# Projections and gated merge of a hybrid decoder block, walked in halves of the tokens instead of in columns of both halves

## The chip, the cores and the metric

The kernel runs on one core of one Trainium2 chip. The metric is device time in microseconds (us) of one execution; a comparison uses the median of several. The engines that matter here are TensorE (PE, with its weight loads PEld), VectorE (DVE), ScalarE (ACT), GpSimd (POOL) and SyncE (SP); SP does no arithmetic here and issues most of the transfers, POOL issues others. Each engine works through its own list of instructions in order: an instruction that waits holds up everything behind it on that engine, the transfers that it would issue included.

## The reference

One decoder block over 1024 tokens of width 1024, in float32:

```python
h = rmsnorm(x, norm1_g)
proj = h @ w_in                       # q, k, v, then u and v of the gating unit, then two gates
gate_a = sigmoid(proj[..., A]); gate_b = sigmoid(proj[..., B])        # 1024 columns each
attn = ...   # dilated attention, three groups mixed: 512 columns
sgu  = ...   # spatial gating unit: 512 columns
merged = gate_a * (attn @ w_proj_attn) + gate_b * (sgu @ w_proj_sgu)  # 512 x 1024 weights each
x = x + merged @ w_out
x = x + (silu(h2 @ w_ffn_gate) * (h2 @ w_ffn_up)) @ w_ffn_down        # h2 = rmsnorm(x, norm2_g)
return rmsnorm(x, final_g)
```

The change concerns the line `merged = ...` and the end of the computation of the two gates just before it.

## The kernel before, in words

Every float32 operand of a product is split into a high part, rounded to the format that TensorE multiplies, and a low part, the rest. `split` (L103 to L105) is one ACT copy (L104, CAST in the profile) and one DVE subtraction (L105). A product takes three matmuls per 128 rows of contraction: high by high, high by low, low by high.

**Gates.** The two gates (8 columns of 128 for each, called c) are computed for both halves of the tokens (512 tokens each) by a scheme that needs seven products in place of eight for each c (`seven`, L803 to L850, driven by the list `order`). A product (c, i) is 12 matmuls of 512 columns. Products 1, 6 and 7 copy their running PSUM sum to a tile `sn` by an ACT copy (L850) before the next product adds to the same bank, which therefore waits for that copy. `gates_after` (L892 to L914) forms the gate values on DVE (L912 among others), applies the sigmoid on ACT (L893) and writes each finished gate, 512 KB for each c and gate, to DRAM by POOL's queue (`put`, L801, in the traces `gate<-go`). Gate weights arrive in tiles `gr`, a ring of 6. On PE the stage ends, as the scheduler placed it, with the products (7,6), (7,5), (7,3) in a bank Z of its own, (7,7) and (7,4).

**Operands of the projections.** The gating unit's output (`sgud`) and the attention's (`attd`) lie in DRAM. `load_side(side, half)` (L940) fetches one side and half in two tiles of 512 KB through SP's queue, and `split_side` (L949) splits them: three of the four (side, half) pairs into the tile `HX`, whose three blocks have been operands of the gate products and come free one after the other, the last pair into a tile `at1` that is made when the merge begins. They pass through the tiles `raw`, a ring of 3.

**Merge.** For each of 8 columns c, for each side (0 is the gating unit, 1 the attention), for each half, there is one projection product: 4 rows of contraction by 3 matmuls, 12 matmuls in a PSUM bank `acc` (3 banks), by `cols_mm` (L351; matmuls on L357 to L359). There are 32 such products. A weight piece ("p", side, c), 256 KB, is loaded by SP into a `raw` tile (L137) and split into a slot of the ring `WH`/`WL`, 8 slots of 512 columns (`need`, `pump`, `load_jobs`); it serves both halves. `load_sg` (L990) fetches both gates of a column, 512 KB each, from DRAM through POOL's queue (L994), one column ahead. DVE multiplies a PSUM bank by the gate (L1006 for side 0, L1008 for side 1), which frees the bank, adds (L1009), and the sum is split into `H`, the left operand of the product with `w_out`, which comes next (matmuls on L344 to L346).

**What sets the order.** A scheduler places each engine's instructions, by the written order, the dependences and `issue_after`, which holds an instruction behind another one. Tiles of one tag share a fixed number of places (`BUFS`); a new tile waits until the old one in its place is no longer used. Pools that open later take the memory of closed ones, so a first write into the new pool also waits for the last use of what lay there: the gate values `sg` lie where gate weights and `go` tiles lay.

## Time and profile before

| What | Value |
|---|---|
| Time, median of 3 runs | 1695.07 us (1692.18 to 1696.88) |
| Profiled execution | 1696.83 us, its span 1695.1 us |
| Mean granted TensorE clock | 0.992 |
| PE busy | 1658.6 us, 98% of the span, 8110 matmuls |
| DVE, ACT, POOL busy | 995.5 us (59%), 709.2 us (42%), 239.4 us (14%) |
| Merge (first to last matmul of L357 to L359) | 856.77 to 957.15 us |

The profile is one execution. A row of a timeline reads: start in us, duration in us, engine, line, operation, tile written and tiles read, repeats, and in brackets the idle time before it on that engine and what ended it. PE's rows begin every 0.23 us though each lasts 0.39, because matmuls overlap; so the time between two starts, not the sum of durations, is what a product costs. A row of windows reads: window, its length, busy time and count for PE, PEld, DVE, ACT and POOL, then the granted TensorE clock, the mean busy share of the 16 DMA engines, and the bytes that they moved in GB/s. Which engine is busiest over the whole says little on one stage; what ended each idle time of PE says where the time can go.

### The profile page before, as it was taken

Reading aid. Unit: us, or ns where it says so; the run is one execution under the profiler, and the core shown is the slowest. Engines: PE = TensorE matmul, PEld = TensorE weight load, DVE = VectorE, ACT = ScalarE, POOL = GpSimd, SP = SyncE. Lnnn points to the kernel's source line nnn. Section 1 sums busy time; section 2 is a strip of 40 time slices with the busy share of each in tenths; the row PEclk is TensorE's granted clock in tenths of the full one; section 3 lists DMA queues with packets and bytes.
Section 4 is the critical chain, followed back from the end, with each engine's and each line's share of the span. In section 5 each row is a group of like instructions: output and inputs, shape, how many; then the busy total and the mean of one; then the engine's idle time right before and its main releaser. Section 6 shows DMA issues by size and latency. Waiting matters only on the chain.

```text
span 1695.1 us, 22401 instructions
## 1 busy us (share of the span) xinstructions
PE 1658.6 (98%) x8110; PEld 1346.8 (79%) x8110; DVE 995.5 (59%) x1868; ACT 709.2 (42%) x1383; POOL 239.4 (14%) x417
## 2 busy tenths in 40 slices
PE   8999999999999999999979999999999999999998
PEld 7877877877887778778858888888888888888886
DVE  5365376366447694665456428776566555565555
ACT  5345435435444563544342116433333333354444
POOL 6200030030012045021010002021000000100003
PEclk9999999999999999999989999999999999999999
DMA  7312331152232224576375514365332322496663
GB/s 216 92 42 70 85 103 50 30 151 55 55 115 75 65 100 132 166 267 224 130 238 179 173 38 149 131 223 190 113 106 95 100 93 94 157 338 231 197 190 111
DMA packets 196239, 227.55 MB, mean 134 GB/s; under 512 B 14561, under 2 KB 141921, under 8 KB 196129
## 3 DMA queue, kind: packets, MB, share of 16 engines
q1 hardware_dynamic: 156624, 135.30, 25.9%
q0 software_dynamic: 24144, 81.38, 13.7%
q10 hardware_dynamic: 15360, 9.45, 2.4%
q8 instruction: 64, 1.05, 0.3%
q14 instruction: 47, 0.38, 0.1%
HBM read 159.52 MB, written 63.41 MB: 132 GB/s over the span
## 4 chain that ended last, share of the span: by engine, by line
PE 60%; issue 9%; DMA 3%; DVE 3%; ACT 1%; POOL 1%; SPq 0%; ACTq 0%; POOLq 0%; DVEq 0%
PE ps_X L845 4%; PE ps_X L847 4%; PE ps_X L846 4%; PE ps_acc L345 4%; PE ps_acc L346 4%; PE ps_acc L344 4%; PE ps_acc L357 3%; PE ps_acc L358 3%; PE ps_acc L359 3%; PE ps_V L847 2%; PE ps_V L846 2%; PE ps_V L845 2%; PE ps_dX L1231 2%; PE ps_dX L1230 2%; PE ps_dX L1229 2%
## 5 line engine op out<-in xcount | busy, mean ns | idle before, releaser
L344 PE MATMUL ps_acc<-WH,H 128*128 128x384 f32 (+1 forms) x512 | 190.6, 374 | 3.6 <-ACT H L104 3.6
L346 PE MATMUL ps_acc<-WH,H 128*128 128x384 f32 (+1 forms) x512 | 191.1, 374 | 0.5 <-DVE H L105 0.5
L345 PE MATMUL ps_acc<-WL,H 128*128 128x384 f32 (+1 forms) x512 | 189.8, 371 | 0.0
L104 ACT CAST WH<-rows 128x512 fp32r<-128x512 f32 x132 | 81.8, 621 | 207.5 <-PE ps_X L846 97.8
L104 ACT CAST WH<-raw 128x512 fp32r<-128x512 f32 (+2 forms) x105 | 85.4, 817 | 178.6 <-PE ps_V L846 48.1
L105 DVE TENSOR_TENSOR WL<-rows,WH 128x512 fp32r<-128x512 f32 x132 | 90.9, 690 | 115.5 <-ACT WH L104 115.5
L359 PE MATMUL ps_acc<-H,WL 128*128 128x512 f32 x384 | 154.0, 401 | 0.0
L357 PE MATMUL ps_acc<-H,WH 128*128 128x512 f32 x384 | 153.8, 400 | 0.0
L358 PE MATMUL ps_acc<-H,WH 128*128 128x512 f32 x384 | 153.3, 399 | 0.0
L845 PE MATMUL ps_X<-H,WH 128*128 128x512 f32 x360 | 141.7, 394 | 3.8 <-ACT sn L850 2.2
L846 PE MATMUL ps_X<-H,WH 128*128 128x512 f32 x360 | 141.5, 393 | 0.0
L847 PE MATMUL ps_X<-H,WL 128*128 128x512 f32 x360 | 138.0, 392 | 0.0
L105 DVE TENSOR_TENSOR WL<-raw,WH 128x512 fp32r<-128x512 f32 (+2 forms) x105 | 97.5, 930 | 42.6 <-ACT WH L104 42.2
L462 ACT ACTIVATE S<-S,sm 128x128 f32<-128x128 f32 (+1 forms) x192 | 84.8, 444 | 70.9 <-DVE sm L460 62.3
L344 PEld LDWEIGHTS ps_acc<-WH,H 128*128 128x128 f32 x512 | 97.1, 190 | 16.4 <-ACT H L104 4.2
L346 PEld LDWEIGHTS ps_acc<-WH,H 128*128 128x128 f32 x512 | 96.9, 189 | 12.6 <-issue 0.9
L345 PEld LDWEIGHTS ps_acc<-WL,H 128*128 128x128 f32 x512 | 96.9, 189 | 11.9 <-issue 0.7
L846 PE MATMUL ps_V<-HX,WH 128*128 128x512 f32 x232 | 91.2, 393 | 0.0
L845 PE MATMUL ps_V<-HX,WH 128*128 128x512 f32 x232 | 91.1, 393 | 0.0
L847 PE MATMUL ps_V<-HX,WL 128*128 128x512 f32 x232 | 91.0, 392 | 0.0
L105 DVE TENSOR_TENSOR WL<-ab,WH 128x512 fp32r<-128x512 f32 x74 | 51.0, 689 | 59.2 <-ACT WH L104 59.2
L359 PEld LDWEIGHTS ps_acc<-H,WL 128*128 128x128 f32 x384 | 72.6, 189 | 16.3 <-issue 0.3
(297 smaller groups left out, 3630.9 us busy)
## 6 DMA issues: line engine op xcount, KB each, us to landing
raw<-in_w_in_dram SPq DMA_DIRECT2D x32, 512.0 KB
raw<-in_w_ffn_down_dram POOLq DMA_DIRECT2D x22, 512.0 KB, 5.3
twd<-raw POOLq DMA_DIRECT2D x22, 512.0 KB, 3.0
rows<-in_w_ffn_gate_dram SPq DMA_DIRECT2D x22, 512.0 KB
rows<-in_w_ffn_up_dram SPq DMA_DIRECT2D x22, 512.0 KB
ab<-twd SPq DMA_DIRECT2D x44, 256.0 KB
gr<-in_w_in_dram SPq DMA_DIRECT2D x16, 512.0 KB
gate<-go POOLq DMA_DIRECT2D x16, 512.0 KB, 4.9
```

Source lines behind the costliest of these rows:

```text
L104: marks["hi"] = nc.scalar.copy(hi, src)
L105: return tt(out=lo, in0=src, in1=fb(hi), op=ALU.subtract)
L344: mm(o, H[:, 0, kt, tok], wh, start=(kt == 0), stop=False)
L345: mm(o, H[:, 0, kt, tok], wl, start=False, stop=False)
L346: mm(o, H[:, 1, kt, tok], wh, start=False, stop=(kt == KT - 1))
L357: mm(ps, WH[:, w], rh, start=(kt == 0), stop=False)
L358: mm(ps, WH[:, w], rl, start=False, stop=False)
L359: mm(ps, WL[:, w], rh, start=False, stop=(kt == n - 1))
L462: nc.scalar.activation(sbt[:, o:o + n], sbt[:, o:o + n], AF.Exp, bias=neg[:, i:i + 1], scale=0.125, accum_out=stt[:, b, 2 + h:3 + h])
L845: mm(ps, WH[:, w], OPS[i](0, k), start=first and k == 0, stop=False, skip_group_check=True)
L846: mm(ps, WH[:, w], OPS[i](1, k), start=False, stop=False, skip_group_check=True)
L847: mm(ps, WL[:, w], OPS[i](0, k), start=False, stop=k == 3, skip_group_check=True)
```

## The change

The merge's loops now run half, then column, then side. Each weight piece is loaded and split once for each half (32 jobs of 256 KB in place of 16). The gate values come as one tile for each half and column that holds both gates, 256 KB each, three steps ahead with four places; those of the first two steps go through SP's queue, placed ahead of the weight pieces that follow, the others stay on POOL's. The operands of half 0 are fetched earlier, into places of the gate weights' ring `gr`, while the last ten products of the gates run; the operands of half 1 are fetched into two tiles `side` in the fourth and sixth step of the merge (n is 3 and 5), and split in the sixth and eighth: the attention's is side 1 with half 1, and takes over the block of `HX` that side 0 of half 0 leaves free. There is no tile `at1`. The first four weight pieces are split before the merge begins. Some `issue_after` orders are added: the operands of side 1 behind those of side 0, splits of later pieces behind the last sum and sigmoid of the gates.

```diff
@@ -72,7 +72,7 @@
     dram = ctx.enter_context(tc.tile_pool(name="dram", bufs=1, space=bass.MemoryType.DRAM))
 
     BUFS = {"A": 4, "qkr": 2, "cs": 2, "vst": 3, "vp": 2, "oT": 3, "att": 2, "raw": 3, "S": 2, "pT": 2, "st": 6,
-            "sm": 8, "cmb": 2, "x2": 8, "y": 2, "sn": 5, "e": 3, "yo": 4, "ab": 6, "go": 4, "gr": 6, "side0": 8, "side1": 8, "sg": 4, "mg": 2, "c": 5}
+            "sm": 8, "cmb": 2, "x2": 8, "y": 2, "sn": 5, "e": 3, "yo": 4, "ab": 6, "go": 4, "gr": 6, "side": 2, "sg": 4, "mg": 2, "c": 5}
     PBUFS = {"acc": 3, "tr": 2, "s": 2, "o": 1, "X": 3, "Y": 2, "V": 2, "Z": 1, "dX": 4, "dV": 3, "dv": 1}
     BASE = {"H", "WH", "WL", "ident", "mhalf", "raw", "sm", "bsT"}
     first_pool = open_pool("mixer")
@@ -121,7 +121,7 @@
     jobs = []
     piece = {}
     live = {}
-    stat = {"load": 0, "split": 0, "at": 0, "raws": 2, "limit": 1 << 30}
+    stat = {"load": 0, "split": 0, "at": 0, "raws": 2, "limit": 1 << 30, "behind": ()}
     raws = {}
     RING = 4096
     AHEAD = 6
@@ -133,8 +133,11 @@
         while stat["load"] < min(len(jobs), stat["limit"]) and stat["load"] < stat["split"] + stat["raws"]:
             key, dmas, shape, n = jobs[stat["load"]]
             t = T_("raw", shape)
-            for dst, src in dmas(t):
-                nc.sync.dma_start(out=dst, in_=src)
+            with ExitStack() as behind:
+                if "sg" in marks:
+                    behind.enter_context(tc.issue_after(marks["sg"].ins))
+                for dst, src in dmas(t):
+                    marks["job"] = nc.sync.dma_start(out=dst, in_=src)
             raws[key] = (t, cur[0])
             stat["load"] += 1
 
@@ -151,7 +154,10 @@
         flat = t if len(shape) == 2 else t.rearrange(f"p {names} -> p ({names})")
         a, ok = room(n)
         assert ok, key
-        split(WH[:, a:a + n], WL[:, a:a + n], flat)
+        with ExitStack() as behind:
+            for ins in stat["behind"]:
+                behind.enter_context(tc.issue_after(ins))
+            split(WH[:, a:a + n], WL[:, a:a + n], flat)
         live[key] = (a, n)
         piece[key] = a
         stat["at"] = a + n
@@ -327,9 +333,10 @@
         for kp in range(4):
             job(("uv", which, kp), one(w_in2[:, 2 * kp:2 * kp + 2, c0:c0 + SGW]), [P, 2, SGW], 1024)
     stat["limit"] = len(jobs)
-    for c in range(KT):
-        for side, wp in enumerate((wps, wpa)):
-            job(("p", side, c), one(wp[:, :, c * P:(c + 1) * P]), [P, 4, P], 512)
+    for half in range(2):
+        for c in range(KT):
+            for side, wp in enumerate((wps, wpa)):
+                job(("p", half, side, c), one(wp[:, :, c * P:(c + 1) * P]), [P, 4, P], 512)
     for ch in range(2):
         for kp in range(4):
             job(("o", ch, kp), one(wo[:, 2 * kp:2 * kp + 2, half_of(ch)]), [P, 2, 512], 1024)
@@ -905,11 +912,11 @@
             if c < KT - 2:
                 load_wd(c, "raw")
         if i == 4:
-            sig(go[c, 0][:, t1], ps)
+            marks["sig"] = sig(go[c, 0][:, t1], ps)
             put(gates_d[0][c], go.pop((c, 0)))
         if i == 3:
             o = go.pop((c, 1))
-            tt(out=o[:, t0], in0=o[:, t0] if last else snap[c, 6], in1=ps, op=ALU.add)
+            marks["add"] = tt(out=o[:, t0], in0=o[:, t0] if last else snap[c, 6], in1=ps, op=ALU.add)
             sig(o[:, t0], o[:, t0])
             put(gates_d[1][c], o)
 
@@ -934,12 +941,12 @@
 
 
     side_raw = {}
-    side_at = {(0, 0): HX[:, 1], (0, 1): HX[:, 0], (1, 0): HX[:, 2]}
+    side_at = {(0, 0): HX[:, 1], (1, 0): HX[:, 0], (0, 1): HX[:, 2], (1, 1): HX[:, 1]}
     side_op = lambda side: lambda kt, half: (side_at[side, half][:, 0, kt], side_at[side, half][:, 1, kt])
 
     def load_side(side, half):
         for q in range(2):
-            t = side_raw[side, half, q] = T_("raw", [P, 2, 512])
+            t = side_raw[side, half, q] = T_("side" if half else "gr", [P, 2, 512])
             if side == 0:
                 nc.sync.dma_start(out=t, in_=sgud[:, 2 * q:2 * q + 2, half_of(half)])
             else:
@@ -950,24 +957,25 @@
         dst = side_at[side, half]
         for q in range(2):
             kk = slice(2 * q, 2 * q + 2)
-            split(dst[:, 0, kk], dst[:, 1, kk], side_raw.pop((side, half, q)))
+            marks["lo"] = split(dst[:, 0, kk], dst[:, 1, kk], side_raw.pop((side, half, q)))
 
     for n, (c, i) in enumerate(order):
         left = len(order) - n
         if n + AHEAD_W < len(order):
             weights(*order[n + AHEAD_W])
-        if left == 7:
-            load_side(0, 0)
-            stat.update(limit=len(jobs), raws=1)
-            load_jobs()
+        if left in (10, 9):
+            load_side(10 - left, 0)
         if left == 4:
             split_side(0, 0)
-            load_side(0, 1)
+            parts = marks["hi"], marks["lo"]
+            stat.update(limit=stat["limit"] + 4, raws=3)
+            load_jobs()
         if left == 3:
+            with tc.issue_after(parts[0].ins), tc.issue_after(parts[1].ins):
+                split_side(1, 0)
             stat["at"] = ring[0] % 8 * 512
-            need(("p", 0, 0))
-        if left == 2:
-            split_side(0, 1)
+            for key in (("p", 0, 0, 0), ("p", 0, 1, 0), ("p", 0, 0, 1), ("p", 0, 1, 1)):
+                need(key)
         product(c, i)
         if i == 7:
             load_gates(c + 3)
@@ -978,36 +986,50 @@
     merge_pool = open_pool("merge")
     PBUFS["tr"] = 5
     merge_psum = open_pool("merge_psum", bass.MemoryType.PSUM)
-    side_at[1, 1] = T_("at1", [P, 2, 4, 512], F32R)
-    T_("pad", [P, 512])
-    load_side(1, 0)
-    split_side(1, 0)
-    load_side(1, 1)
-    split_side(1, 1)
-    stat["raws"] = BUFS["raw"]
+    T_("pad", [P, 4608])
+    stat.update(limit=len(jobs), behind=(marks["sig"].ins, marks["add"].ins))
     sg = {}
 
-    def load_sg(c):
-        if c < KT:
-            sg[c] = [T_("sg", [P, S]) for _ in range(2)]
-            for j in range(2):
-                nc.gpsimd.dma_start(out=sg[c][1 - j], in_=gates_d[1 - j][c])
-
-    load_sg(0)
-    for c in range(KT):
-        load_sg(c + 1)
-        m = T_("mg", [P, S])
-        for side in range(2):
-            for half in range(2):
+    def load_sg(n):
+        if n < 2 * KT:
+            half, c = divmod(n, KT)
+            sg[n] = T_("sg", [P, 2, 512])
+            for j in (1, 0):
+                queue = nc.sync if n < 2 else nc.gpsimd
+                load = queue.dma_start(out=sg[n][:, j], in_=gates_d[j][c][:, half_of(half)])
+                if n < 2:
+                    marks["sg"] = load
+
+    for n in range(BUFS["sg"] - 1):
+        load_sg(n)
+    load_jobs()
+    for half in range(2):
+        for c in range(KT):
+            n = KT * half + c
+            load_sg(n + BUFS["sg"] - 1)
+            if n == 2:
+                stat["behind"] = ()
+                del marks["sg"]
+            if n == 3:
+                with tc.issue_after(marks["job"].ins):
+                    load_side(0, 1)
+            if n == 5:
+                with tc.issue_after(marks["hi"].ins), tc.issue_after(marks["mg"].ins):
+                    split_side(0, 1)
+                load_side(1, 1)
+            m = T_("mg", [P, 512])
+            for side in range(2):
                 pp = PS("acc")
-                cols_mm(pp, ("p", side, c), 4, side_op(side), half, half == 1)
-                gt, mh = sg[c][1 - side][:, half_of(half)], m[:, half_of(half)]
+                cols_mm(pp, ("p", half, side, c), 4, side_op(side), half, True)
+                gt = sg[n][:, 1 - side]
                 if side == 0:
-                    tt(out=mh, in0=gt, in1=pp, op=ALU.mult)
+                    tt(out=m, in0=gt, in1=pp, op=ALU.mult)
+                    if n == KT - 1:
+                        split_side(1, 1)
                 else:
                     tt(out=gt, in0=gt, in1=pp, op=ALU.mult)
-                    tt(out=mh, in0=mh, in1=gt, op=ALU.add)
-                    split(H[:, 0, c, half_of(half)], H[:, 1, c, half_of(half)], mh)
+                    tt(out=m, in0=m, in1=gt, op=ALU.add)
+                    marks["mg"] = split(H[:, 0, c, half_of(half)], H[:, 1, c, half_of(half)], m)
     close_pool(merge_pool)
     close_pool(extra_pool)
 
```

PE has the same matmuls in both kernels. The first place where the order of the other engines moves is SP's queue from the last gate weights on. Here L944 and L947 (L951 and L954 of the changed kernel) fetch operands, L137 (L140) a weight piece, L999 gate values. Before:

```order
L944 DMA raw_1014_7385<-sgud_5306 128x2x512
L944 DMA raw_1015_7387<-sgud_5306 128x2x512
L137 DMA raw_1016_7389<-in_w_proj_sgu_dram 128x4x128
L944 DMA raw_1020_7442<-sgud_5306 128x2x512
L944 DMA raw_1021_7444<-sgud_5306 128x2x512
L137 DMA raw_1023_7461<-in_w_proj_attn_dram 128x4x128
L947 DMA raw_1029_7525<-attd0_81 128x512
...
L947 DMA raw_1032_7538<-attd3_84 128x512
L137 DMA raw_1040_7577<-in_w_proj_sgu_dram 128x4x128
```

After:

```order
L951 DMA gr_1010_7327<-sgud_5306 128x2x512
L951 DMA gr_1011_7329<-sgud_5306 128x2x512
L954 DMA gr_1014_7356<-attd0_81 128x512
...
L954 DMA gr_1015_7359<-attd3_84 128x512
L140 DMA raw_1021_7446<-in_w_proj_sgu_dram 128x4x128
L140 DMA raw_1022_7448<-in_w_proj_attn_dram 128x4x128
L140 DMA raw_1023_7450<-in_w_proj_sgu_dram 128x4x128
L140 DMA raw_1025_7471<-in_w_proj_attn_dram 128x4x128
L999 DMA sg_1030_7536<-gate1_0_6317 128x512
...
L999 DMA sg_1031_7539<-gate0_1_6310 128x512
L140 DMA raw_1033_7545<-in_w_proj_sgu_dram 128x4x128
```

Both lists begin behind the last load of gate weights. In the second, half 0's operands and four weight pieces come first, then the gate values of two steps; the twelve transfers of operands of the first list are six, and the other half's follow later.

The second place is ACT around the two copies to `sn` (L850, L857 of the changed kernel) that the last two products of the gates wait for. Before:

```order
L893 ACTIVATE go_1011_7341<-go_1011_7341 128x512
L104 CAST HX_909_6350<-raw_1014_7385 128x1024
L850 COPY sn_1019_7436<-ps_X_1012_7352 128x512
L104 CAST HX_909_6350<-raw_1015_7387 128x1024
L850 COPY sn_1024_7475<-ps_X_1012_7352 128x512
```

After:

```order
L900 ACTIVATE go_1013_7345<-go_1013_7345 128x512
L104 CAST HX_909_6350<-gr_1010_7327 128x1024
L104 CAST WH_2_67<-raw_1025_7471 128x512
L857 COPY sn_1020_7440<-ps_X_1016_7362 128x512
L104 CAST HX_909_6350<-gr_1011_7329 128x1024
L104 CAST HX_909_6350<-gr_1014_7356 128x1024
L104 CAST HX_909_6350<-gr_1015_7359 128x1024
L857 COPY sn_1026_7491<-ps_X_1016_7362 128x512
```

The casts of operands stand around the copies in both; in the second they read `gr` tiles, and a weight piece's cast stands ahead of the first copy.

The third place is DVE where the gates end and the merge begins: L1006, L1008 and L1009 (L1026, L1030 and L1031) are the merge's multiplications and addition. Before:

```order
L912 TENSOR_TENSOR go_1025_7477<-go_1025_7477,ps_Z_1026_7485 128x512
L105 TENSOR_TENSOR WL_3_68<-raw_1023_7461,WH_2_67 128x512
L105 TENSOR_TENSOR HX_909_6350<-raw_1029_7525,HX_909_6350 128x1024
L105 TENSOR_TENSOR HX_909_6350<-raw_1030_7528,HX_909_6350 128x1024
L105 TENSOR_TENSOR at1_1027_7523<-raw_1031_7535,at1_1027_7523 128x1024
L105 TENSOR_TENSOR at1_1027_7523<-raw_1032_7538,at1_1027_7523 128x1024
L105 TENSOR_TENSOR WL_3_68<-raw_1040_7577,WH_2_67 128x512
L1006 TENSOR_TENSOR mg_1037_7553<-sg_1034_7546,ps_acc_1038_7554 128x512
```

After:

```order
L919 TENSOR_TENSOR go_1027_7493<-go_1027_7493,ps_Z_1028_7497 128x512
L1026 TENSOR_TENSOR mg_1037_7554<-sg_1030_7536,ps_acc_1038_7555 128x512
L1030 TENSOR_TENSOR sg_1030_7536<-sg_1030_7536,ps_acc_1039_7569 128x512
L1031 TENSOR_TENSOR mg_1037_7554<-mg_1037_7554,sg_1030_7536 128x512
L1026 TENSOR_TENSOR mg_1044_7601<-sg_1031_7539,ps_acc_1045_7602 128x512
L105 TENSOR_TENSOR H_1_66<-mg_1037_7554,H_1_66 128x512
L105 TENSOR_TENSOR WL_3_68<-raw_1033_7545,WH_2_67 128x512
```

Before, six splits stand between the gates' last sum and the merge's first multiplication, the last of them that of a weight piece; now the first multiplication follows the gates' last sum, and the first split of a weight piece comes after three multiplications.

## The prediction

> **What bounds the kernel now.** I read the page first, then PE's waits, then windows and timelines around the largest wait. PE's first row of the page and the head of its waits:
>
> ```profile
> PE 1658.6 (98%) x8110; PEld 1346.8 (79%) x8110; DVE 995.5 (59%) x1868; ACT 709.2 (42%) x1383; POOL 239.4 (14%) x417
> PE ps_acc L357 <- DVE mg L1006: 9.8, 1, 9.8
> ...
> PE ps_X L845 <- ACT sn L850: 2.2, 3, 0.8
> ```
>
> PE bounds the kernel, and the change leaves its matmuls as they are; only PE's waits, and half-clock stretches behind them, can be won. One wait stands out: a merge matmul (L357) waited 9.8 us, once, for the first multiplication by a gate (L1006). PE's timeline from the last gate products to the first product with `w_out`:
>
> ```profile
> 849.01 0.40 PE L847 MATMUL ps_Z<-HX,WL 128*128 128x512 f32 x1
> 850.22 0.50 PE L845 MATMUL ps_X<-H,WH 128*128 128x512 f32 x1 [0.81 <-ACT sn L850]
> 852.85 0.39 PE L847 MATMUL ps_X<-H,WL 128*128 128x512 f32 x1
> 853.91 0.50 PE L845 MATMUL ps_X<-H,WH 128*128 128x512 f32 x1 [0.68 <-ACT sn L850]
> 856.77 0.40 PE L357 MATMUL ps_acc<-HX,WH 128*128 128x512 f32 x1
> 864.79 0.40 PE L359 MATMUL ps_acc<-HX,WL 128*128 128x512 f32 x1
> 874.95 0.77 PE L357 MATMUL ps_acc<-at,WH 128*128 128x512 f32 x1 [9.76 <-DVE mg L1006]
> 880.21 0.43 PE L357 MATMUL ps_acc<-HX,WH 128*128 128x512 f32 x1
> 957.15 0.39 PE L344 MATMUL ps_acc<-WH,H 128*128 128x512 f32 x1
> ```
>
> From 880.21 to 957.15 run 28 of the 32 merge products: 76.94 / 28 = 2.748 us each, 0.229 per matmul. By that pace the Z product could have been followed at 849.24, and two gate products and 32 merge products would take 34 x 2.748 = 93.43 us; they took 957.15 - 849.24 = 107.91. So 14.5 us are lost here, and no more can be won: 850.22 - 849.24 = 0.98 before (7,7); 0.83 before (7,4), 853.91 less 852.85 + 0.23; 0.11 in each of these two products, slow to start (853.91 to 856.77 is 2.86); 874.95 - 865.02 = 9.93, where 865.02 is 864.79 + 0.23, the end of three products, as many as there are banks; and the fourth product, 874.95 to 880.21, 5.26 - 2.75 = 2.51 too long. The windows say why that product is long, and what the DMA engines did (clock, DMA share and GB/s are the last three numbers):
>
> ```profile
> 865.00:868.00 3.00, 0.19 (x1) 0.00 (x0) 1.23 (x1) 0.61 (x2) 0.53 (x1) 1.00 1.03 407
> 868.00:872.00 4.00, 0.00 (x0) 0.00 (x0) 1.23 (x1) 0.96 (x1) 0.00 (x0) 0.76 1.05 386
> 875.00:878.00 3.00, 3.00 (x7) 2.40 (x8) 2.88 (x5) 1.24 (x3) 0.53 (x1) 0.50 0.62 145
> 880.00:957.00 77.00, 77.00 (x337) 63.13 (x337) 47.50 (x71) 17.77 (x27) 6.34 (x12) 1.00 0.51 155
> ```
>
> After the gap PE had half its clock (0.50); during it all 16 DMA engines were full. The chain of waits tells what L1006 waited for:
>
> ```profile
> 862.48 10.36 DMA raw<-in_w_proj_sgu_dram
> 872.86 0.63 ACT WH L104
> 874.12 0.69 DVE mg L1006
> ```
>
> The multiplication's own inputs were not the last to come: it stood in DVE's order behind the split of the third weight piece, whose 256 KB took 10.36 us through the full DMA engines. And the piece was asked for only at 862.48, since its `raw` tile went through two rounds of operands first.
>
> **The change part by part.** *The 9.93 us.* In the new order of DVE the first multiplication stands directly behind the gates' last sum, and four pieces are split before. It then hangs on its gate values. The rows on them:
>
> ```profile
> 849.05 0.53 POOL L801 DMA_DIRECT2D gate<-go  x1 [5.69 <-ACT go L893]
> 858.45 1.05 POOL L801 DMA_DIRECT2D gate<-go  x2 [8.87 <-ACT go L893]
> 866.61 0.53 POOL L994 DMA_DIRECT2D sg<-gate  x1 [5.53 <-DMA gate<-go]
> gate<-go POOLq DMA_DIRECT2D x16, 512.0 KB, 4.9
> DMA to landing us min/median/max: 3.7/4.8/10.6
> ```
>
> The last row is of the tile `sg`, 512 KB a load. The first `sg` tile now lies where the second-last column's `go` lay, so its load needs that `put` landed: 849.05 + 4.9 = 853.95 at the latest if nothing else moves, some 2 us sooner if its sigmoid no longer stands behind a cast of operands (below). The merge would start at 856.77 - 0.98 = 855.79 and want its first bank again three products later, at 864.03; with 0.69 for the multiplication and 0.14 to PE, the gate values are due at 863.2. Between 853.95 and 863.2 are 9.2 us. The load costs between 3.7 and 10.6 (512 KB in quiet and in the burst; it is now 256 KB twice), so it is 5.5 us early or, at worst, 1.4 us late. I take early: the burst is thinned, since half 1's operands and half of the gate bytes move out of it, and the fifth piece waits behind these loads on SP. The second tile's loads follow on SP without another wait of that kind. The third comes by POOL behind the last two `put`s (859.5), with product 7's bank at 855.79 + 7 x 2.748 = 875.0 to meet: 859.5 + 10.6 is 5 us before. The fourth needs the last `put`, landed by 866.6: 877.2 at worst against 880.5.
>
> What is queued behind SP's wait for that `put`: the fifth piece. Asked for at 854 to 855, it lands by 865.4 even at 10.36, and with a cast (0.62) and a subtraction (0.69) is there at 866.7; the fifth product begins at 855.79 + 4 x 2.748 = 866.8. Just in time at the worst price, 7 us early at a quiet one. So 9.93 goes, and with no gap the 2.51 of half clock go too.
>
> *The 0.98 us.* ACT around the copies to `sn`:
>
> ```profile
> 847.17 1.05 ACT L104 CAST HX<-raw 128x1024 fp32r<-128x1024 f32 x1 [4.64 <-DMA raw<-sgud]
> 848.12 0.63 ACT L893 ACTIVATE go<-go 128x512 f32<-128x512 f32 x1
> 848.66 1.03 ACT L104 CAST HX<-raw 128x1024 fp32r<-128x1024 f32 x1
> 849.60 0.57 ACT L850 COPY sn<-ps_X 128x512 f32<-128x512 f32 x1
> 853.27 0.59 ACT L850 COPY sn<-ps_X 128x512 f32<-128x512 f32 x1 [2.15 <-PE ps_X L847]
> 814.15 0.69 DVE L105 TENSOR_TENSOR WL<-gr,WH 128x512 fp32r<-128x512 f32 x1 [2.04 <-ACT WH L104]
> 845.32 0.69 DVE L912 TENSOR_TENSOR go<-sn,ps_V 128x512 f32<-128x512 f32 x1 [2.56 <-PE ps_V L847]
> ```
>
> A cast waited 4.64 us for operands, and behind it came a sigmoid whose sum was done at 846.01 (845.32 + 0.69), a second cast, and the first copy. In the new order two casts still stand between sigmoid and copy, of an operand tile and of the fourth piece. The operand's place, in the ring `gr`, is free once the last gate weights are split, at 814.84 (814.15 + 0.69), some 30 us ahead. The fourth piece takes the tile of the first, whose split stands ahead of that sum on DVE, so done by the start of the 2.56 idle, 842.76; with a load of 3.56 (row below) it is there at 846.3. From 846.05: sigmoid 0.6, casts 1.05 and 0.62, to 848.3; the copy's 0.57 ends at 848.9, before 849.24. The gain is 0.98; at worst 0, where the piece is late. The second copy follows PE itself (2.15 idle until PE's last matmul), so 0.83 and the 0.11s stay.
>
> *The 16 added pieces.* Each is a load of 256 KB, a cast and a subtraction; the rows of the window 880.2 to 957.15 with 28 products, and one load with its cast:
>
> ```profile
> L105 DVE TENSOR_TENSOR WL<-raw,WH 128x512 fp32r<-128x512 f32 x12 | 8.2, 685 | 2.0 <-ACT WH L104 2.0
> L104 ACT CAST WH<-raw 128x512 fp32r<-128x512 f32 x10 | 6.2, 622 | 11.3 <-DMA raw<-in_w_proj_sgu_dram 5.9 <-PE ps_acc L358 4.2 <-DMA raw<-in_w_proj_attn_dram 1.2
> 884.51 0.37 SPq L137 DMA_DIRECT2D raw<-in_w_proj_sgu_dram  x1
> 888.07 0.62 ACT L104 CAST WH<-raw 128x512 fp32r<-128x512 f32 x1 [2.95 <-DMA raw<-in_w_proj_sgu_dram]
> 861.23 1.24 DVE HX L105
> ```
>
> DVE was busy 47.50 / 28 = 1.70 us per product. One subtraction per product in place of half a one adds 0.34; half 1's four operand splits (1.24 each, now inside the merge) add 0.15: 2.19 of 2.748, 80%. ACT: 17.77 / 28 = 0.63, plus 0.31 and 0.13, 39%. All of it lies beside PE; without that cover 16 x (0.62 + 0.69) = 21 us would show. DMA: 155 GB/s at a share of 0.51; 16 x 0.26 MB of pieces and 2.1 MB of operands add 6.3 MB over some 88 us, 72 GB/s, so a share near 0.75. A piece's tile is taken for 3.56 (884.51 to 888.07) + 0.62 + 0.69 = 4.9 us; three tiles serve one product each, so 3 x 2.748 = 8.24 are allowed. Nothing, then, from a quiet load; the other end is the second rival. I put 1 us down for casts and subtractions waiting in order now and then, between 0 and the 8 us of the rival's lower end.
>
> *Half 1's operands.* Side 1's overwrite the block that the 15th product reads last, free at 855.79 + 15 x 2.748 = 897.0; two casts and two subtractions overlap to about 1.06 + 2 x 1.24 = 3.5, so 900.5 against the 18th product at 902.5: hidden with 2 us left, which three foreign DVE instructions of 0.69 ahead would use up. Cost 0, at most about 2. Behind the last product the halves of `H` are finished earlier than before, so `w_out` starts without a wait, as now.
>
> *Sum.* 9.93 + 2.51 + 0.98 = 13.42, less 1.0: 12.4. The profiled execution took 1696.83, 1.76 above the median, so it becomes 1684.4, and on the median 1695.07 - 12.4 = 1682.7.
>
> **The rivals.** *1. Part of the stall stays (14%).* The first gate values are late by 1.4 us (load at its worst), or by 3 if the `put` too is slow by 1.7. A short gap may bring half clock with it:
>
> ```profile
> 695.05 0.50 PE L845 MATMUL ps_X<-H,WH 128*128 128x512 f32 x1 [1.62 <-ACT WH L104]
> 695.90:699.40 3.50, 3.50 (x10) 2.73 (x9) 3.40 (x6) 1.66 (x3) 0.00 (x0) 0.51 0.41 117
> ```
>
> A gap of 1.62 us was followed by 3.5 us at 0.51, half of which is lost, 1.75. So 1.4 to 3 plus 1.75 at most: 1684 to 1687.5. For it speaks that SP, a queue with everything behind it, now holds these loads; against it, 9.2 us of room.
>
> The Trainium skill, "TensorE: Matmul & The Clock Gate", Part 1, puts the half rate behind an idle window of about 3.4 us; by it a wait of 3 us would cost no clock and rival 1 would end at 1685.7. The trace disagrees with its 1.62, and the measurement decides.
>
> *2. The other side: the three `raw` tiles become the bound (12%; slower than before in 5%).* If a load takes long under the added traffic, a product can't start more often than L / 3, L being load, cast, subtraction and what they wait for. From L = 8.24 it costs (L / 3 - 2.748) x 32; at 9.5 the whole 13.4 us are given back; at the burst's 10.36 + 1.31 = 11.7 it is +36.8 us, 1719. For it: the fullest windows above run at 386 to 407 GB/s, and ACT already waited 7.1 us for pieces (row of L104). Against: a share of 0.75 is not 1.03, and 3.4 us are to spare. With L near 9 it would give 1690.
>
> The Trainium skill, "DMA: Bandwidth & Descriptors", Bandwidth, asks for transfers of 1 MiB and more; this change halves the gate loads and doubles the pieces' count. By its fit of 2.0 us plus bytes an estimate for 256 KB is 2.6 us, below the 3.56 measured, so it too leaves rival 2 unlikely.
>
> *3. Half 1's operands are late (8%).* PE waits up to 2 us before the 18th product, with 1.75 of clock: 1684.5 to 1686.5.
>
> *4. The wait only moves (5%).* The pieces were late before because `raw` served operands too; were the last `put`s and the SP queue the true limit, the first multiplication would wait about as long as now and the time stay near 1695. Against: the fourth `sg` load, the latest, was issued at 866.61 and L1006 did not wait for it.
>
> **How the numbers follow.** Forecast 61%, 1682.7, its own range 1679.5 (all but the 1 us of copies that follow PE is won, and the runs' scatter) to 1685. Rivals 1 and 3 are still faster by over 0.3%, which is what a measurement of this kernel can tell from no change, 5.1 us, below 1690; of rival 2, 3% is faster, 4% within and 5% slower. Faster 0.61 + 0.14 + 0.08 + 0.03 = 0.86; same 0.05 + 0.04 = 0.09; slower 0.05. The range 1679 to 1690 leaves out some of each of rivals 2 and 4.
>
> **What would show it.** Right: no wait of PE on the merge's first multiplication, clock 1.00 from the first merge product on; first merge matmul within 1 us behind the gates at its pace, `w_out` about 88 us after it; only one wait of 0.7 for `sn` left. Rival 1: the fourth merge matmul group waits with `sg` as the DMA before it. Rival 2: several waits of PE on L104 or L105 of `WH`, spread over the merge, with DMA shares near 1. Rival 3: one wait near the 18th product, behind a split of `HX`. The forecast is wrong if the stretch from the Z product to `w_out` is longer than about 98 us, or if time is lost in a stage that the change doesn't touch.

## The result, and the profile after

The changed kernel takes 1687.6 us in the median of 5 runs (1684.66 to 1688.52), the kernel before 1695.26 (5 runs, 1692.18 to 1696.88). The ratio is 0.9945 with an interval of 0.9935 to 0.9956: faster by 0.0055 x 1695.26 = 9.3 us (7.5 to 11.0; the two medians differ by 7.7), where 12.4 was forecast. The interval leaves out 1, so the gain is clear of the scatter.

PE's waits, the head of that view after:

```profile
PE ps_tr L212 <- DVE H L105: 4.2, 2, 3.9
...
PE ps_X L852 <- ACT sn L857: 1.4, 2, 0.7
PE ps_acc L364 <- DVE sg L1030: 1.1, 1, 1.1
...
PE ps_acc L365 <- DVE HX L105: 0.2, 1, 0.2
```

The 9.8 us for the first multiplication are gone. (The first row lies at 34 us, in a stage that both kernels share.) Two small waits stand in the merge that were not there: 1.1 us for a multiplication of the attention's side (L1030), and 0.2 for an operand block. PE's timeline after, at the places that the prediction used:

```profile
850.68 0.39 PE L854 MATMUL ps_Z<-HX,WL 128*128 128x512 f32 x1
854.49 0.50 PE L852 MATMUL ps_X<-H,WH 128*128 128x512 f32 x1 [0.68 <-ACT sn L857]
857.35 0.40 PE L364 MATMUL ps_acc<-HX,WH 128*128 128x512 f32 x1
891.63 0.47 PE L364 MATMUL ps_acc<-HX,WH 128*128 128x512 f32 x1 [1.14 <-DVE sg L1030]
907.40 0.50 PE L365 MATMUL ps_acc<-HX,WH 128*128 128x512 f32 x1 [0.17 <-DVE HX L105]
947.16 0.40 PE L351 MATMUL ps_acc<-WH,H 128*128 128x512 f32 x1
```

From the last matmul of Z to the first product with `w_out` (the **stretch** in what follows) it took 957.15 - 849.01 = 108.14 before and 947.16 - 850.68 = 96.48 now: 11.66 less. Z to the merge is 6.67 instead of 7.76: the first wait for `sn` is gone, with its slow start of 0.11. The 32 merge products take 89.81 instead of 100.38, where 32 x 2.748 = 87.94 would do.

The first multiplication waited for PE, not for its gate values, and the DMA engines are no longer full where PE stood still (DVE's timeline, then windows; both of the changed kernel):

```profile
860.31 0.69 DVE L1026 TENSOR_TENSOR mg<-sg,ps_acc 128x512 f32<-128x512 f32 x1 [3.56 <-PE ps_acc L366]
```

```profile
865.00:868.00 3.00, 3.00 (x15) 2.46 (x14) 1.89 (x3) 1.70 (x4) 0.84 (x2) 1.00 0.77 262
868.00:872.00 4.00, 4.00 (x19) 3.28 (x18) 3.36 (x6) 1.14 (x2) 1.03 (x2) 1.00 0.44 135
880.00:892.00 12.00, 10.86 (x48) 8.62 (x47) 6.75 (x11) 4.25 (x7) 1.06 (x2) 1.00 0.78 234
892.00:910.00 18.00, 17.83 (x78) 14.20 (x77) 16.69 (x25) 9.72 (x14) 3.19 (x6) 1.00 0.88 278
910.00:947.00 37.00, 37.00 (x164) 30.34 (x163) 27.56 (x42) 12.59 (x19) 5.85 (x11) 1.00 0.66 204
```

From 865 to 872 the share fell from 1.03 and 1.05 to 0.77 and 0.44. The burst is not gone but comes earlier: the share is 1.00 from 855 to 860 and 0.88 from there to 865, while PE waits for nothing. The two waits lie in the stretch from 880 to 910, where the share rises again and half 1's operands come in. The chain of waits around them:

```profile
885.16 4.29 DMA raw<-in_w_proj_attn_dram
...
890.20 0.03 DVE WL L105
...
890.81 0.69 DVE sg L1030
...
898.12 5.80 DMA raw<-in_w_proj_sgu_dram
...
903.99 0.09 ACT WH L104
...
904.52 0.61 ACT H L104
905.13 0.96 ACT HX L104
...
906.12 1.24 DVE HX L105
```

It is the old stall in small: a multiplication stands in DVE's order behind the split of a weight piece whose load took 4.29 us; then the casts of half 1's operands stand in ACT's order behind a piece whose load took 5.80.

### The profile page after: what moved, and what is told of

Read it like the earlier page. It is cut to its first block, busy times and chain, and to the rows that moved or that the text cites. A ratio compares the mean times of both kernels' runs of the same rounds, so it can differ in the third digit from the quotient of the medians.

```text
span 1685.9 us, 22540 instructions
## 1 busy us (share of the span) xinstructions
PE 1657.1 (98%) x8110; PEld 1345.5 (80%) x8110; DVE 1001.6 (59%) x1884; ACT 718.0 (43%) x1399; POOL 245.6 (15%) x429
## 3 DMA queue, kind: packets, MB, share of 16 engines
q8 instruction: 64, 1.05, 0.3%
## 4 chain that ended last, share of the span: by engine, by line
PE 45%; issue 18%; DVE 6%; DMA 4%; ACT 2%; POOL 1%; ACTq 0%; SPq 0%; POOLq 0%; DVEq 0%
PE ps_acc L352 3%; PE ps_acc L351 3%; PE ps_acc L353 3%; PE ps_X L852 3%; PE ps_X L854 3%; PE ps_X L853 3%; PE ps_acc L364 3%; PE ps_acc L366 3%; PE ps_acc L365 3%; PE ps_dX L1252 2%; PE ps_dX L1251 2%; PE ps_dX L1253 2%; PE ps_dV L1253 1%; PE ps_V L852 1%; PE ps_V L853 1%
## 5 line engine op out<-in xcount | busy, mean ns | idle before, releaser
L104 ACT CAST WH<-raw 128x512 fp32r<-128x512 f32 (+2 forms) x121 | 95.0, 791 | 200.9 <-PE ps_V L853 51.2
L104 ACT CAST WH<-rows 128x512 fp32r<-128x512 f32 x132 | 81.8, 621 | 207.3 <-PE ps_X L853 97.6
L105 DVE TENSOR_TENSOR WL<-raw,WH 128x512 fp32r<-128x512 f32 (+2 forms) x121 | 108.1, 897 | 48.5 <-ACT WH L104 48.3
L351 PEld LDWEIGHTS ps_acc<-WH,H 128*128 128x128 f32 x512 | 97.6, 191 | 15.2 <-ACT H L104 2.9
L352 PEld LDWEIGHTS ps_acc<-WL,H 128*128 128x128 f32 x512 | 97.3, 190 | 11.8 <-issue 0.7
```

The costliest lines, as they stand in the source:

```text
L104: marks["hi"] = nc.scalar.copy(hi, src)
L105: return tt(out=lo, in0=src, in1=fb(hi), op=ALU.subtract)
L351: mm(o, H[:, 0, kt, tok], wh, start=(kt == 0), stop=False)
L352: mm(o, H[:, 0, kt, tok], wl, start=False, stop=False)
```

## The experiments

All are compared with the kernel before; "stretch" is from one profile of each. "Lost in the merge" is the 32 products' time less 87.94. The runs came in four batches, in which the kernel before had medians of 1695.04 to 1697.14, so rows are best compared by their ratios.

| Kernel | Median, us | Ratio (95% interval) | Stretch, us | Lost in the merge, us |
|---|---|---|---|---|
| before / once more | 1695.26 / 1696.03 | 1 / 1.0002 (0.9992 to 1.0012) | 108.1 / 107.5 | 12.4 / 11.5 |
| changed / once more | 1687.6 / 1686.89 | 0.9945 / 0.9942 (0.9929 to 0.9955) | 96.5 / 98.1 | 1.9 / 3.5 |
| six places for pieces | 1687.71 | 0.9946 (0.9933 to 0.9959) | 99.6 | 5.0, all behind the wait for the 6th piece |
| first gate values on POOL | 1693.67 | 0.9983 (0.9974 to 0.9992) | 105.6 | 11.0 |
| no early staging | 1691.72 | 0.9966 (0.9953 to 0.9979) | 101.6 | 4.3 |
| one piece split early | 1688.88 | 0.9958 (0.9943 to 0.9973) | 100.0 | 5.4 |
| before, piece behind the multiplication | 1693.14 | 0.9978 (0.9969 to 0.9988) | 104.8 | 8.9 |
| two places for pieces | 1686.6 | 0.9941 (0.9926 to 0.9956) | 97.2 | 2.6 |
| six places from the 8th piece on | 1685.32 | 0.9941 (0.9929 to 0.9953) | 96.4 | 1.7 |
| on POOL, splits held behind | 1690.49 | 0.9969 (0.9956 to 0.9983) | 98.8 | 0.5 |
| later splits | 1684.84 | 0.9937 (0.9926 to 0.9949) | 96.8 | 2.1 |
| later splits, operands earlier | 1685.53 | 0.9942 (0.9929 to 0.9956) | 97.6 | 3.0 |

**Both kernels once more.** The same code, for a second profile.

> The changed kernel once more, unaltered, with a second profile. In the first pair of profiles the stretch from the last matmul of the Z product to the first product with w_out fell from 108.1 to 96.5 us, while PE reached that place 1.7 us later than in the kernel before, though all engines' orders are equal up to there. Theory A (those 1.7 us are scatter between executions): the stretch is again 96 to 97, but the lag before it differs by 1 us or more from 1.7, and the median stays between 1684 and 1689. Theory B (the changed program is slower ahead of the merge, by another place of its code or data): the lag repeats within 0.3 us.

> The kernel before once more, unaltered, for a second profile. Theory A (scatter between executions ahead of the merge): its stretch from Z to w_out is again 108 us within 1, but the time at which it reaches the last Z matmul differs from the first profile's 849.0 by 1 us or more. Theory B (a given program repeats there): 849.0 within 0.3 us.

The last Z matmul, in the changed kernel's second profile, came at 848.18 instead of 850.68, and in the second of the kernel before at 848.16 instead of 849.01. Theory A holds in substance: ahead of the merge, executions of one program differ by 0.9 and 2.5 us, the first just short of the 1 us that it named (over all profiles of this study, whose matmuls are the same up to there, Z comes between 845.7 and 850.7). The 1.7 us by which the first pair of profiles differed is within that. The stretch itself moves too, against Theory A's 96 to 97: 98.1 instead of 96.5, since the same two waits were longer:

```profile
889.45 0.47 PE L364 MATMUL ps_acc<-HX,WH 128*128 128x512 f32 x1 [1.46 <-DVE sg L1030]
906.50 0.50 PE L365 MATMUL ps_acc<-HX,WH 128*128 128x512 f32 x1 [0.75 <-DVE HX L105]
```

The mean stretch of the two profiles of each kernel falls from 107.8 to 97.3, by 10.5 us, which fits the 9.3 timed.

**The order alone, on the kernel before.** The third piece's split is held behind the multiplication that it blocked.

```diff
+            if key == ("p", 0, 1):
+                behind.enter_context(tc.issue_after(marks["mult"].ins))
...
+        if key == ("p", 0, 1) and "mult" not in marks:
+            return
...
+                    mult = tt(out=mh, in0=gt, in1=pp, op=ALU.mult)
+                    marks.setdefault("mult", mult)
```

> The kernel before with one edit: the split of the third weight piece, in which the first multiplication was stuck, is held behind that multiplication (and its cast on ACT is where it was). Theory (the order on DVE was only the last of several late things; the third piece itself, landed at 872.8, is needed two products later): the first multiplication runs at about 870, PE starts again some 4 us earlier, then waits for the third piece at the fifth product; 1 to 3 us faster than before. Rival (the order alone made the stall): the full 12 us are won.

The chain of this kernel shows who is late next:

```profile
856.26 8.26 DMA raw<-attd
...
864.54 1.05 ACT at L104
...
866.76 0.69 DVE mg L1011
```

The wait fell from 9.76 to 5.42 us, the stretch by 3, the time by 3.7 us (2.0 to 5.3). The rival falls: behind the piece stood the splits of the attention's half 1, whose load took 8.26. So it is not one order but the list of late loads ahead of the first multiplication, and the change had to take all of it away. That the third piece would make a second wait at the fifth product was wrong: by then it had come.

**No early staging.** Half 0's operands pass through the three `raw` tiles again, the rest is as changed.

```diff
-        if left in (10, 9):
-            load_side(10 - left, 0)
+        if left == 7:
+            load_side(0, 0)
...
-            stat.update(limit=stat["limit"] + 4, raws=3)
-            load_jobs()
+            load_side(1, 0)
...
                 split_side(1, 0)
+            stat.update(limit=stat["limit"] + 4, raws=3)
+            load_jobs()
...
-            t = side_raw[side, half, q] = T_("side" if half else "gr", [P, 2, 512])
+            t = side_raw[side, half, q] = T_("side" if half else "raw", [P, 2, 512])
```

> The changed kernel without the early staging: half 0's operands pass through the three raw tiles, as before the change, ahead of the four pieces. Theory (the third piece was late because the raw tiles served operands first): four pieces now stand on DVE ahead of the first multiplication, asked for only once operands are split; the first sn wait of 0.9 to 1 us is back, PE waits 3 to 8 us in the first products of the merge, the kernel gives back 4 to 9 us. Rival (the half-first order alone, which takes half 1's 2 MB of operands and half of the gate bytes out of the burst, did it): gives back at most the 1 us of the sn wait.

Measured: 4.1 us given back by the medians (1691.72 - 1687.6; 4.8 against the changed kernel's 1686.89 of the same batch), 2.7 of them ahead of the merge (Z to merge 9.41 instead of 6.67):

```profile
854.69 0.69 PE L852 MATMUL ps_X<-H,WH 128*128 128x512 f32 x1 [1.82 <-ACT sn L857]
```

The rival's "at most 1 us" is passed, but the first products lost 0.6 us rather than 3 to 8: the half-first order, with four pieces split first and the first gate values on SP as changed, already spares the merge most of the stall. Staging is worth the `sn` wait with its half clock, and 0.8 to 2.4 us of merge. No run has the half-first order without those two other parts, so its own share is not measured.

**One piece instead of four split ahead of the merge.**

```diff
-            stat.update(limit=stat["limit"] + 4, raws=3)
+            stat.update(limit=stat["limit"] + 1, raws=3)
-            for key in (("p", 0, 0, 0), ("p", 0, 1, 0), ("p", 0, 0, 1), ("p", 0, 1, 1)):
-                need(key)
+            need(("p", 0, 0, 0))
```

> The changed kernel with one weight piece instead of four split ahead of the merge; the others follow behind the gate values on SP, and on DVE four splits then stand between the first and the second multiplication. Theory (pieces asked for early are half of the gain): second piece asked for at about 852 lands by 857 and is split by 858.5 if the order allows; the stretch from Z to w_out grows by 2 to 5 us. Rival (DMA is quiet enough that pieces land in 4 us anyway): within 1 us of the changed kernel.

The stretch grew to 100.0, by 1.9 and 3.5 against the two profiles of the changed kernel, in six waits of 0.4 to 0.9 us spread from the second to the 18th product; the medians differ by 1.3, not clear of the scatter. Direction as in the theory, a small part.

**The first gate values on POOL.**

```diff
-                queue = nc.sync if n < 2 else nc.gpsimd
+                queue = nc.gpsimd
```

> The changed kernel with the first two steps' gate values on the POOL queue, behind the last puts of the gates, instead of SP. The scheduler then sets six splits of weight pieces ahead of the first multiplication on DVE instead of none. Theory (what stands ahead of the first multiplication in DVE's order decides, together with when its gate values are asked for, 859 instead of 851.6): PE waits at the fourth merge product again: gate values at 859.5 + 4 to 5 = 864, the sixth piece behind at about 869 to 872, so 5 to 8 us of wait plus about 2 us of half clock; the kernel gives back 6 to 10 us of its gain. Rival (the queue does not matter since bandwidth is what was short, and now it isn't): within 1 us of the changed kernel.

Most of the gain went: 1693.67 us. The scheduler, which expected the gate values later, had put six splits of pieces ahead of the first multiplication; its chain of waits is the old one again:

```profile
857.60 11.42 DMA raw<-in_w_proj_attn_dram
...
869.10 0.63 ACT WH L104
...
870.35 0.69 DVE mg L1026
...
871.09 0.79 PE ps_acc L364
```

From 857.6 to 869 the DMA engines were full again (a share of 1.05). So is it the queue or the order? The next kernel keeps POOL and restores the order.

**On POOL, splits held behind.** Pieces from the fifth on are split behind the second step's first multiplication.

```diff
-                queue = nc.sync if n < 2 else nc.gpsimd
+                queue = nc.gpsimd
...
+        if "hold" in marks:
+            return
         if cur[0] - raws[key][1] < AHEAD or not room(n)[1]:
...
+    marks["hold"] = True
...
-                    tt(out=m, in0=gt, in1=pp, op=ALU.mult)
+                    mult = tt(out=m, in0=gt, in1=pp, op=ALU.mult)
+                    if n == 1:
+                        del marks["hold"]
+                        stat["behind"] = (mult.ins,)
```

> The kernel with the first gate values on POOL (which took the stretch to 105.6 us) with the splits of the fifth and later pieces held behind the second step's first multiplication, as the changed kernel has it. Theory (DVE's order made most of that loss: the first multiplication stood behind the split of the ninth or so piece, whose load took 11.4 us): what is left is the later request for the gate values, 7.5 us, of which some 5 were spare; stretch 97 to 100. Rival (the queue itself made it): stretch 103 or more.

In this profile the merge lost 0.5 us, the least of all, with the first gate values on POOL: the later request by itself cost PE nothing there. It took most of the spare time, though: the first multiplication waited for its gate values until 865.88 and was done 1.0 us before PE wanted the bank (867.7, three products behind 859.48, with 0.14 to PE). And holding the splits also holds the loads behind them: no piece was asked for between 850.54 and 869.74, where the kernel above asked for five between 856.39 and 865.43, and the DMA share was 0.78 from 861 to 866. So what the edit took away is the order on DVE together with the burst of loads; the two are not told apart. ACT's order had moved as well: two casts of pieces stood ahead of the second copy to `sn`, and a new wait with half clock came before the merge:

```profile
853.55 1.14 ACT L104 CAST WH<-raw 128x512 fp32r<-128x512 f32 x2 [1.05 <-DMA raw<-in_w_proj_sgu_dram]
854.60 0.58 ACT L859 COPY sn<-ps_X 128x512 f32<-128x512 f32 x1
```

```profile
855.23 0.79 PE L854 MATMUL ps_X<-H,WH 128*128 128x512 f32 x1 [2.48 <-ACT sn L859]
```

Its profiled execution was among its faster ones (1687.63, the median 1690.49), so the 98.8 flatters it; that most of the loss on POOL was order, with the loads that follow from it, rests on the profiles.

**How many places for pieces.** Two in place of three, then six (`pr`, in the pad), then six from the eighth piece on.

```diff
-        while stat["load"] < min(len(jobs), stat["limit"]) and stat["load"] < stat["split"] + stat["raws"]:
+        while stat["load"] < min(len(jobs), stat["limit"]):
             key, dmas, shape, n = jobs[stat["load"]]
+            two = "two" in marks and key[0] == "p"
+            if stat["load"] >= stat["split"] + (2 if two else stat["raws"]):
+                break
...
+    marks["two"] = True
```

> The changed kernel with two of the three raw tiles in use for the merge's pieces. A place is taken for load, cast, subtraction and their waits in order. Theory (ring of places bounds the merge: places x 2.748 us must cover that time; in the changed kernel's merge a load alone took 4.3 to 5.2 us where PE waited): with two places 5.5 us are allowed, against 4.5 + 1.3 = 5.8 or more, so PE waits throughout: (5.8 to 7) / 2 - 2.748 = 0.15 to 0.75 us per product, 4 to 21 us over 28 products; slower than the changed kernel by that. Rival (a load takes 3.5 us unless several collide): within 2 us of the changed kernel.

```diff
...
-            t = T_("raw", shape)
+            if stat["load"] >= stat["split"] + (6 if six else stat["raws"]):
+                break
+            t = T_("pr" if six else "raw", shape)
...
-    T_("pad", [P, 4608])
+    T_("pr", [P, 4, P])
+    T_("pad", [P, 1536])
```

> The changed kernel with six places instead of three for the merge's weight pieces (in the unused pad). Theory (the waits of 1.14 and 0.17 us that PE still has in the merge come from pieces asked for too late, since a place must come free first; the second rival of the prediction in small): they go, the stretch from Z to w_out falls from 96.5 to about 94.9, the kernel is 1 to 2 us faster than the changed one. Rival (DMA bandwidth is the limit, 228 GB/s at a share of 0.73 in the merge): loads that start earlier only take longer, the stretch stays at 96 to 97.

> The changed kernel with six places for the merge's weight pieces from the eighth piece on (the first seven pass through the three raw tiles). With six places from the fifth piece on, the waits around the 11th to 18th product were gone, but the sixth piece's place lay over gate tiles and came free only at 862.7, which cost 5 us at the fifth product. Theory (the late waits come from loads asked for too late): no wait near the fifth product now, none later; the stretch from Z to w_out falls from 96.5 and 98.1 to 94.5 to 95.5, and the time by 1 to 3 us. Rival (the early stall merely gave later loads time to get ahead): the waits of 1.1 and 0.2 to 0.8 us are back, stretch 96 to 98.

Two places cost nothing: 2.6 us lost in the merge, against 1.9 and 3.5 with three. My steady bound, places x 2.748 us against the time that a place is taken, is wrong here. A ring that was the bound would have lost 4 to 21. Six places from the fifth piece on took every late wait away, but cost as much early: the sixth piece's place lay over gate tiles, was asked for at 862.68 and took 6.30 us to come. Six from the eighth piece on kept one wait, for half 1's operands:

```profile
903.99 0.74 PE L368 MATMUL ps_acc<-HX,WH 128*128 128x512 f32 x2 [1.46 <-ACT HX L104]
```

Its chain leads to their load, 6.21 us, asked for at 896.5. The wait near the 13th product is gone there, as the theory had it; the wait for operands was not foreseen, and the gain of 1 to 3 us is not clear of the scatter (1685.32 and 0.9941).

**Later splits, and operands earlier.**

```diff
-        if cur[0] - raws[key][1] < AHEAD or not room(n)[1]:
+        if cur[0] - raws[key][1] < (8 if key[0] == "p" else AHEAD) or not room(n)[1]:
```

> The changed kernel with one number: in the merge a piece is split at the earliest 8 instead of 6 steps of contraction (0.69 us each) behind its load in the written order, so the scheduler may set the split later on ACT and DVE. Theory (loads take 4.3 to 5.2 us where the order plans for 6 x 0.69 = 4.1, and multiplications stand behind such a split): the wait of 1.1 to 1.5 us near the 14th product goes, the stretch falls by 1 to 2 us. Rival (it is the number of places or bandwidth): the wait stays, or moves to the piece itself, stretch 96 to 98.

The wait near the 14th product fell to 0.34, that at the 18th stayed at 0.58; the merge lost 2.1, and the stretch of 96.8 is no clear fall from 96.5 and 98.1. With half 1's attention operands in two places of their own (`side1`, in the pad), asked for at n = 4:

> The changed kernel with the later split of pieces (8 steps instead of 6, which brought the wait near the 14th product from 1.1 to 1.5 down to 0.3 us) and with half 1's attention operands in two places of their own in the pad, so that they are asked for one step earlier (n is 4 instead of 5). Theory (the wait at the 18th product comes from these operands being asked for late, 895 us, and from a piece's late load ahead of their casts on ACT): it goes too, the merge's 32 products take 88 to 89 us and the stretch from Z to w_out 94.7 to 95.7, 1 to 3 us faster than the changed kernel. Rival (the DMA engines are the limit around there, at a share of 0.88): the wait stays at 0.5 to 1.5 us or moves to a piece.

It went as the rival had it, with a stretch of 97.6: the wait at the 18th product fell to 0.19, but two others came ahead of the 14th and 15th:

```profile
PE ps_acc L364 <- DVE mg L1029: 1.1, 1, 1.1
PE ps_acc L364 <- DVE sg L1033: 0.5, 1, 0.5
```

The chain ahead of the first names a piece whose load took 6.44 us. Of the variants, later splits alone has the lowest median, 1684.84; its interval overlaps the changed kernel's, so no version is shown to beat it.

What these leave **open** is what sets the last 2 to 3 us. With two, three and six places, with splits later and operands earlier, the merge lost 1.7 to 3.5 us, always from the 13th to the 18th product. Three kernels of this form had almost none there (six places, and the two on POOL), and in all three PE had lost 3.7 to 11 us before. That fits transfers as the pace of this stretch (share 0.78 to 0.88 in the changed kernel, loads of 4.3 to 6.6 us where PE waited), and an early wait just gives them a lead. Against it, the kernel without early staging lost 2.7 us ahead of the merge and still waited 0.7, 1.3 and 0.8 us from the 14th to the 18th product. No run took bytes out of it, so this is argued, not shown.

## Why the prediction was right, point by point

- **Where it landed.** 1687.6 is inside the range of 1679 to 1690, but 2.6 us above the forecast's own 1679.5 to 1685; it is a time that the rivals had been given, and rival 3, at 8%, did come in part. Of the signs, the stretch of "about 98 us" above which the forecast would be wrong was kept by 96.5 in one profile and touched by 98.1 in the other.
- **The place and the mechanism: right.** "So 9.93 goes, and with no gap the 2.51 of half clock go too": both went. The first multiplication's gate values were in time, asked for at 851.6, and DVE sat idle 3.56 us until PE was done. Rivals 1 and 4 fall. The 2.51 was the size of one execution: in the second profile of the kernel before, the wait was as long (9.84), and the fourth product, 874.51 to 878.74, was 1.48 too long.
- **The 0.98 us: right.** Z to the merge fell by 1.09, 0.98 and 0.11; the second `sn` wait stayed at 0.68, as said. One of the two 0.11s went with the first wait, where I had both staying.
- **The term that was mis-sized** is "1 us down for casts and subtractions waiting in order", together with "Cost 0, at most about 2" for half 1's operands. The merge lost 1.9 and 3.5 us in two profiles: 1.3 and 1.6 near the 13th product, where a multiplication waits behind a piece, and 0.4 and 1.5 at the 18th, rival 3. The 2 us of spare that I counted for half 1 were taken by its attention load, asked for only at 895, and by a piece's cast ahead of it on ACT.
- **Rival 2 in the form given: wrong.** Where PE waited, a load took 4.3 to 6.6 us instead of 3.56; with cast and subtraction that is 5.6 to 7.9, still below the 8.24 that three places allow, and places are not the bound: two do as well as three. The waits come one at a time, from the order on DVE and ACT, under transfers that take longer at a share of 0.88. I had the mean share right (0.75 forecast; 228 GB/s at 0.73 from 860 to 947, as this row of windows says) and missed that it is not even:

```profile
860.00:947.00 87.00, 85.69 (x374) 69.58 (x373) 63.75 (x96) 32.38 (x50) 14.47 (x28) 1.00 0.73 228
```

- **The sum.** 13.4 less 2.7, the mean lost in the merge, is 10.7; the two profiles of each kernel give 10.5, the timing 9.3 (7.5 to 11.0). Of what the 12.4 was too much, 1.7 is the part of those waits beyond the 1.0 put down. From the first product with `w_out` to the end of the span, both profiles of the changed kernel also take 0.7 us longer (738.7 against 738.0), all of it behind the last arithmetic instruction; no run shows why. What is left lies within the timing's interval.

## What to carry to other kernels

When an engine's first use in a new stage comes late, list everything that stands ahead of it in its own order, not only the last releaser: moving one split won 3.7 of the 9.3 us, since the next late load was right behind it. Where a scheduler plans with expected landing times, moving a load to another queue also moves the order of engines that never touch that queue; look at those orders, and at the loads that they let start, before blaming the queue. A mean DMA share well below 1 does not price a burst inside the stage; take the share of the stretch in which the operands of the next phase come in.

## What the runs showed of the hardware that was not expected

A gap of PE far shorter than 3.5 us can be followed by some 3.5 us at half the granted clock. Windows behind three gaps, of 1.46 us (six places from the 8th piece on), 1.82 (no early staging) and 2.48 (on POOL, splits held behind); the clock is the third number from the end:

```profile
903.90:907.40 3.50, 3.41 (x15) 2.81 (x16) 2.94 (x4) 1.28 (x3) 0.00 (x0) 1.00 1.09 319
```

```profile
854.60:858.10 3.50, 3.41 (x8) 2.73 (x9) 3.50 (x6) 1.88 (x4) 0.00 (x0) 0.53 0.31 93
```

```profile
855.10:858.60 3.50, 3.37 (x9) 2.71 (x10) 1.97 (x3) 1.34 (x3) 0.36 (x1) 0.55 0.02 5
```

The length of the gap alone does not decide it. In all 14 profiles a matmul of the gates, near 695 us, waits 1.61 or 1.62 us for the cast of a weight piece. In nine of them the clock then falls to 0.50, as in the prediction's row of the kernel before; in five it stays at 1.00, as in the second profile of that same kernel:

```profile
694.88 0.50 PE L845 MATMUL ps_X<-H,WH 128*128 128x512 f32 x1 [1.61 <-ACT WH L104]
```

```profile
695.70:699.20 3.50, 3.50 (x17) 2.85 (x16) 3.40 (x6) 2.41 (x5) 0.00 (x0) 1.00 0.42 119
```

Nor is a shorter gap safe: with six places from the 8th piece on, one of 1.46 us was followed within 2 us by one of 0.92, and the 3.5 us from there ran at 0.51. So these profiles give no length as a threshold, and what else decides they do not show. Where it came behind a short gap, the half clock cost about 1.6 to 1.7 us beyond the gap itself (3.5 us at 0.51 to 0.55). The Trainium skill, "TensorE: Matmul & The Clock Gate", Part 1, names an idle window of about 3.4 us; these runs had the half rate behind gaps of half that, in some executions and not in others, and the measurement decides.
